# Attention's diagonal mask moved to TensorE, its shifts and biases to ScalarE, meta tokens in pieces, output weights split ahead, early Newton steps on GpSimd

## The chip, the cores and the metric

The kernel runs on one core of one Trainium2 chip. The metric is the device time of one execution in microseconds (us); three runs of the kernel before gave 3083.47, 3087.96 and 3088.3. The engines are PE (TensorE, with its weight loads), DVE (VectorE), ACT (ScalarE), POOL (GpSimd) and SP (SyncE, which issues nearly all DMAs here).

## The reference

One layer of a hybrid encoder over T = 2064 tokens (16 learned meta tokens and 2048 of input), width 1024, float32:

```python
p = rms_norm(h, g1) @ w_in                       # columns for three head groups
oa = rg_lru_group(...)                           # 256 wide, a linear recurrence
ob = forgetting_attention_group(q, k, v, f)      # 8 heads of 64
oc = rwkv7_group(...)                            # 256 wide, a matrix recurrence
h += rms_norm(concat(oa, ob, oc) @ w_out, g2)
f = causal_dwconv3(rms_norm(h, g3) @ ffn_up)     # 2 x 2816 columns
h += rms_norm((gelu(gate) * val) @ ffn_down, g4)

# attention of one head, c = cumsum(log_sigmoid(f + bias)):
s = q @ k.T + (c[:, None] - c[None, :])          # q scaled by 1/8
p = softmax(where(kpos <= qpos, s, -inf)); o = p @ v
```

The meta tokens are dropped at the end.

## The kernel before, in words

**Stages.** The projection runs in three parts of tokens, each over all 24 column groups ("units", 25 turns of a loop in a part); float32 operands are split into a high and a low float32r part and multiplied in three products (`mm3`, L166). Weights are split in the first part and kept in DRAM scratch for the other two. Beside it run the recurrences, sums for the up projection (`up_sums`, at every second unit of parts two and three, its DMAs queued behind the unit's weight load by `issue_after`), and, at the end, the recurrences' tail overlaps attention. Then come attention (`Attn`), the output projection by token tiles (`w_out_tile`: tile 0 has two meta tokens, sixteen more have 128 rows), the up projection and the down projection.

**What sets the order.** Each engine executes its own queue in order. The queues are filled by a planner that takes instructions by the program's order as priority and by a model of their times, so later work whose data is ready fills places that earlier work leaves: output tiles 0 to 6 stand among attention's second half. `issue_after` pins an instruction behind another in its queue. Tiles 7 and 8 are held until attention is nearly through.

**Attention.** Two halves: token blocks 0 and 1 for all eight heads, then blocks 2 and 3. One step is one head and one block of 512 queries, in two passes. `maxima` multiplies each of four query tiles with keys in pieces of at most 512 columns (L545, PSUM tile `mx`, two banks, three from head 5 of the first half on), and DVE reduces each piece to a column of `mc` (L548); the diagonal's last 128 columns go through a DVE operation that adds the mask `future` and takes the maximum, with a read of its accumulator (L551). Then DVE makes the shift column `sh` (L558, L559), PE transposes it (L563), DVE writes it into four rows of `q2` (L574), against four rows of ones in the keys, and DVE makes the bias of the exponentials (L566). `weights` makes scores (L673, L674), exponentials on ACT (L678, nine buffers `p`), values (L696) and denominators, added three times in four on POOL (L717). Maxima run two steps ahead of weights. `tick` counts clock steps, one per two key tiles, and at given delays runs the denominator's DMA round trip (`scr_den`, `dcol`, `rb`).

**Meta tokens.** `meta` computes attention of the first 16 tokens for all heads in one go between the two halves, in five of the nine `p` buffers.

**Output projection.** `w_out_load` loads eight slices of 512 KB, splits each by ACT (L162) and DVE (L163) and keeps them, once the recurrences' memory is free. A tile's two PSUM banks are squared and summed by ACT, `rstd_from` (L85 to L90) finds the reciprocal root by three Newton rounds of two DVE operations on one column, and DVE scales and adds; a second such norm follows for the next stage. From tile 8 on, `rstd_root` takes a square root on ACT instead.

## Time and profile before

| | |
|---|---|
| median of three runs | 3087.96 us (3083.47 to 3088.3) |
| profiled execution | 3087.03 us, span 3085.3 us |
| PE busy | 2905.6 us, 94% |
| DVE busy | 2127.9 us, 69% |
| ACT busy | 1447.5 us, 47% |
| POOL busy | 1317.4 us, 43% |
| mean granted PE clock | 0.964 |

The profile is one execution. A row of a grouped view reads: line, engine, operation, output<-inputs, shapes, count | busy us, mean ns of one | idle time of the engine just before, and who ended it. A row of waits reads: who waited <- for whom: us in total, times, longest. A busy PE may be waiting inside its pipeline, since the ends of its matmuls are modelled. The stages are about: projection to 885 us, attention to 1600, remaining output tiles to 1715, up projection to 2600, down projection to the end.

### The profile page before, as it was taken

How to read it: one execution, taken by the hardware profiler on the slowest of the kernel's cores; microseconds unless marked ns; L12 is line 12 of the kernel's file. 1: busy time of each engine (PE TensorE's matmuls, PEld its weight loads, DVE VectorE, ACT ScalarE, POOL GpSimd, SP SyncE). 2: the span in 40 equal slices, each digit the busy share in tenths (PEclk: the TensorE clock that was granted, in tenths of full speed). 3: DMA queues.
4: the chain of work that ended last, by engine and by line, in shares of the span. 5: the costliest groups of instructions: out<-in, count | busy, mean ns of one | idle time of the engine just before them, and what ended most of it. 6: DMA issues, size and time to landing. Idle time of an engine off the chain costs nothing.

```text
span 3085.3 us, 52708 instructions
## 1 busy us (share of the span) xinstructions
PE 2905.6 (94%) x18470; PEld 2485.8 (81%) x18470; DVE 2127.9 (69%) x4349; ACT 1447.5 (47%) x2783; POOL 1317.4 (43%) x1491
## 2 busy tenths in 40 slices
PE   7999999999989878898989899999999999999998
PEld 6998899888866544565458899999999998787876
DVE  5268544766677867777745788788778776547766
ACT  4245322444335534445534656666566665324333
POOL 1001121122134645546742457445645534556665
PEclk9999999999978979999999999999999999999999
DMA  6776457466653345445235555566777765435444
GB/s 216 244 229 215 148 176 221 153 219 219 192 134 78 91 112 126 109 112 119 61 112 185 166 175 176 178 196 213 216 211 212 217 193 164 167 103 174 145 163 143
DMA packets 463210, 515.78 MB, mean 167 GB/s; under 512 B 84977, under 2 KB 355003, under 8 KB 461393
## 3 DMA queue, kind: packets, MB, share of 16 engines
q1 hardware_dynamic: 462560, 512.03, 55.5%
q8 instruction: 145, 2.38, 0.3%
q14 instruction: 121, 0.98, 0.1%
q0 software_dynamic: 384, 0.39, 0.0%
HBM read 360.73 MB, written 151.56 MB: 166 GB/s over the span
## 4 chain that ended last, share of the span: by engine, by line
PE 39%; DMA 5%; DVE 5%; POOL 3%; issue 2%; ACT 1%; SPq 0%; POOLq 0%; DVEq 0%; ACTq 0%
PE psu L168 9%; PE psu L169 9%; PE psu L170 8%; PE psd L170 2%; PE psd L169 2%; PE psd L168 2%; DMA u<-scr_ff 1%; PE po L696 1%; DMA xt<-scr_h 1%; PE pswo L168 1%; PE pswo L169 1%; PE pswo L170 1%; DVE fo L1571 1%; PE sc L673 1%; DVE uw L1571 1%
## 5 line engine op out<-in xcount | busy, mean ns | idle before, releaser
L168 PE MATMUL psu<-xo,uw 128*128 128x344 f32 x1848 | 591.3, 324 | 16.2 <-ACT xo L1570 6.9
L169 PE MATMUL psu<-xo,uw 128*128 128x344 f32 x1848 | 594.1, 322 | 0.5 <-DVE xo L1571 0.5
L170 PE MATMUL psu<-xo,uw 128*128 128x344 f32 x1848 | 584.3, 320 | 0.0
L170 PE MATMUL psp<-xh,wl 128*128 128x384 f32 (+2 forms) x1152 | 379.1, 330 | 3.8 <-DMA wl<-scr_wk 3.8
L168 PE MATMUL psp<-xh,wh 128*128 128x384 f32 (+2 forms) x1152 | 380.2, 330 | 2.3 <-DMA wh<-scr_wk 2.3
L169 PE MATMUL psp<-xl,wh 128*128 128x384 f32 (+2 forms) x1152 | 377.6, 328 | 0.0
L168 PEld LDWEIGHTS psu<-xo,uw 128*128 128x128 f32 x1848 | 348.1, 189 | 19.5 <-ACT xo L1570 7.1
L1571 DVE TENSOR_TENSOR uw<-uq,uw 128x512 fp32r<-128x512 f32 x341 | 311.1, 918 | 65.3 <-ACT uw L1570 62.4
L169 PEld LDWEIGHTS psu<-xo,uw 128*128 128x128 f32 x1848 | 349.2, 189 | 1.1 <-DVE xo L1571 1.0
L170 PEld LDWEIGHTS psu<-xo,uw 128*128 128x128 f32 x1848 | 347.6, 189 | 0.0
L1570 ACT ACTIVATE uw<-uq 128x512 fp32r<-128x512 f32 x462 | 288.0, 627 | 113.0 <-PE psu L170 53.8
L678 ACT ACTIVATE p<-sc,bias 128x512 f32<-128x512 f32 (+4 forms) x352 | 197.8, 590 | 238.2 <-PE sc L674 181.7
L1701 DVE SCALAR_TENSOR_TENSOR uy<-psu,ffn_cols,uy 128x342 f32<-128x342 f32 (+1 forms) x396 | 223.8, 566 | 67.3 <-ACT uy L1699 65.9
L717 POOL TENSOR_TENSOR acc<-acc,p 128x512 f32<-128x512 f32 (+3 forms) x208 | 223.8, 1082 | 65.2 <-DVE acc L717 40.4
L1707 POOL TENSOR_TENSOR uy<-uy,uy 128x342 f32<-128x342 f32 (+1 forms) x132 | 138.5, 1049 | 256.3 <-DVE uy L1701 72.1
L170 PEld LDWEIGHTS psp<-xh,wl 128*128 128x128 f32 x1152 | 219.5, 191 | 13.3 <-issue 6.3
L1571 POOL TENSOR_TENSOR uw<-uq,uw 128x512 fp32r<-128x512 f32 x121 | 175.6, 1451 | 125.9 <-ACT uw L1570 102.8
L168 PEld LDWEIGHTS psp<-xh,wh 128*128 128x128 f32 x1152 | 219.6, 191 | 8.5 <-issue 3.5
L169 PEld LDWEIGHTS psp<-xl,wh 128*128 128x128 f32 x1152 | 219.3, 190 | 6.8 <-issue 4.8
L548 DVE TENSOR_REDUCE mc<-mx 128x1 f32<-128x400 f32 (+6 forms) x320 | 171.7, 553 | 67.3 <-PE mx L545 62.5
L1571 DVE TENSOR_TENSOR fo<-u,fo 128x896 fp32r<-128x896 f32 x88 | 109.7, 1247 | 122.4 <-ACT fo L1570 122.4
L1570 ACT ACTIVATE fo<-u 128x896 fp32r<-128x896 f32 x88 | 81.1, 922 | 206.2 <-POOL u L1817 111.7
(460 smaller groups left out, 6474.0 us busy)
## 6 DMA issues: line engine op xcount, KB each, us to landing
uq<-scr_us SPq DMA_DIRECT2D x220, 256.0 KB
uq<-in_ffn_up_dram SPq DMA_DIRECT2D x209, 256.0 KB
wl<-scr_wk SPq DMA_DIRECT2D x48, 512.0 KB
wh<-scr_wk SPq DMA_DIRECT2D x48, 512.0 KB
u<-scr_ff SPq DMA_DIRECT2D x88, 256.0 KB
scr_ff<-uy SPq DMA_DIRECT2D x110, 171.0 KB
raw<-in_w_in_dram SPq DMA_DIRECT2D x24, 512.0 KB
scr_wk<-wh SPq DMA_DIRECT2D x24, 512.0 KB
```

The costliest lines, as they stand in the source:

```text
L168: nc.tensor.matmul(out, ah, bh, start=first, stop=False, skip_group_check=more)
L169: nc.tensor.matmul(out, ah, bl, start=False, stop=False, skip_group_check=more)
L170: nc.tensor.matmul(out, al, bh, start=False, stop=last, skip_group_check=more)
L548: self.reduced = nc.vector.tensor_reduce(mc[:rows, i, ci : ci + 1], ps[:rows, :full], axis=AX.X, op=ALU.max)
L673: nc.tensor.matmul(ps[:rows, :w], k1[:, ks : ks + rows], q1[:, c0:n], start=True, stop=False)
L678: last = nc.scalar.activation(p[:rows, :w], ps[:rows, :w], AF.Exp, bias=bias[:rows, j : j + 1])
L696: mm = nc.tensor.matmul(po[at : at + 64, c0:n], v1[:rows, j], p[:rows, : n - c0], start=start and i < 2, stop=end and i + 2 >= len(group), ...
L717: eng.tensor_tensor(a, ps_[0][0][:rows, c0:n] if start and i == 1 else a, p[:rows, : n - c0], op=ALU.add)
L1570: core.nc.scalar.activation(hi, src, AF.Copy)
L1571: (eng or core.nc.vector).tensor_tensor(lo, src, hi, op=ALU.subtract)
L1701: stt(y[:, :n], src[:, i : n + i], cw[:, 44 * i + cc : 44 * i + cc + 1], y[:, :n], op0=ALU.mult, op1=ALU.add)
L1707: core.pooled = nc.gpsimd.tensor_tensor(v[:, :n], g[:, :n], v[:, :n], op=ALU.mult)
```

## The change

- **Mask.** The last piece of a query tile gets a second matmul, a bfloat16 identity times a bfloat16 mask, into its last 128 columns; DVE reduces the whole piece. The mask operation, its accumulator read and `junk` go. Where the diagonal is a piece of its own, a reduction takes the place of the mask operation alone.
- **Shift.** `sh` is the plain maximum; four transposes put its columns side by side into one row, and one ACT operation negates it, subtracts the reference (`ncref`) and writes one row of `q2`. One row of ones in the keys instead of four.
- **Bias.** The same expression on ACT.
- **Meta tokens.** `meta` is a generator of six pieces, advanced at every odd clock step, in tiles of its own, which lie below a `pad` of the size of the output stage's memory.
- **Output weights.** `w_out_split` loads and splits them in the projection's second part, at odd units, and stores both parts in scratch; `w_out_load` issues 16 loads.
- **Newton steps.** With `core.apart` (output tiles 0 to 7), the six steps of `rstd_from` run on GpSimd.

```diff
@@ rstd_from
+        if apart:
+            nc.gpsimd.tensor_scalar(t, y, hx, y, op0=ALU.mult, op1=ALU.mult)
+            nc.gpsimd.tensor_scalar(y, t, 1.5, y, op0=ALU.add, op1=ALU.mult)
+            continue
         stt(t, y, hx, y, op0=ALU.mult, op1=ALU.mult)
         stt(y, t, 1.5, y, op0=ALU.add, op1=ALU.mult)
@@ attn_consts, gate_block
+    core.futureb, core.identb = (c.tile([P, P], BF16, name=s) for s in ("futureb", "identb"))
...
+    nc.scalar.activation(core.ncref[:, js].rearrange("p j h -> p (j h)"), ps[0:1, :w], AF.Copy, scale=-1.0)
@@ Attn
-    ONES = 4
+    ONES = 1
@@ maxima
-                ps = self.mx()
-                nc.tensor.matmul(ps[:rows, : e - a], q3[:, qo : qo + rows], k2[:, a:e], start=True, stop=True)
-                full = min(e, prior) - a
-                if full > 0:
-                    self.reduced = nc.vector.tensor_reduce(mc[:rows, i, ci : ci + 1], ps[:rows, :full], axis=AX.X, op=ALU.max)
-                if e == prior + rows:
-                    junk = self.t([P, P], "mj")
-                    nc.vector.tensor_tensor_reduce(
-                        junk[:rows, :rows], ps[:rows, full : full + rows], core.future[:rows, :rows],
-                        1.0, NEG, ALU.add, ALU.max, mc[:rows, i, 5:6],
+                ps, last = self.mx(), e == prior + rows
+                nc.tensor.matmul(ps[:rows, : e - a], q3[:, qo : qo + rows], k2[:, a:e], start=True, stop=not last)
+                if last:
+                    nc.tensor.matmul(
+                        ps[:rows, prior - a : e - a], core.identb[:], core.futureb[:], start=False, stop=True
                     )
+                self.reduced = nc.vector.tensor_reduce(
+                    mc[:rows, i, ci : ci + 1], ps[:rows, : e - a], axis=AX.X, op=ALU.max
+                )
                 yield None
         sh = self.t([P, 4], "sh")
-        rows = qt[0][1]
-        nc.vector.tensor_reduce(sh[:rows, :nq], mc[:rows, :nq], axis=AX.X, op=ALU.max)
-        nc.vector.tensor_scalar(
-            sh[:rows, :nq], sh[:rows, :nq], -1.0, core.cref[:rows, ref, h : h + 1], op0=ALU.mult, op1=ALU.subtract
-        )
+        nc.vector.tensor_reduce(sh[:], mc[:], axis=AX.X, op=ALU.max)
         ps = self.mx()
-        nc.tensor.transpose(ps[:nq, :rows], sh[:rows, :nq], core.ident[:rows, :rows])
-        self.shift(q2.rearrange("p (i q) -> p i q", q=P), ps[:nq, :rows])
+        for i in range(nq):
+            nc.tensor.transpose(ps[0:1, P * i : P * i + P], sh[:, i : i + 1], core.ident[:])
+        nc.scalar.activation(q2[64:65], ps[0:1], AF.Identity, scale=-1.0, bias=core.ncref[:, ref, h : h + 1])
         bias = self.t([P, NKT], "bias", bufs=self.AHEAD + 1)
-        nc.vector.tensor_scalar(
-            bias[:], core.ccol[:, :, h], -1.0, core.cref[:, ref, h : h + 1], op0=ALU.mult, op1=ALU.add
+        nc.scalar.activation(
+            bias[:], core.ccol[:, :, h], AF.Identity, scale=-1.0, bias=core.cref[:, ref, h : h + 1]
         )
@@ meta
-        new = lambda shape, dt: self.t(shape, "p", dt, self.NP)
+        new = lambda shape, dt: pool.tile(shape, dt, name=core.n("mt"), tag=core.n("mt"))
...
+        yield
@@ tick
+        if self.clock % 2:
+            with self.core.tc.issue_after(self.reduced.ins):
+                next(self.beside, None)
@@ run
-                self.meta()
+                self.beside = self.meta(pool)
@@ w_out
+def w_out_split(core, pool, w_out, scr):
+
+    for k in range(KD):
+        hi, lo = (pool.tile([P, D], F32R, tag="nt_x", name=core.n("wo")) for _ in range(2))
+        load_parts(core, (pool, "nt_x", None), w_out[k * P : (k + 1) * P, :], hi[:], lo[:])
+        for i, t in enumerate((hi, lo)):
+            core.nc.sync.dma_start(scr["wo"][k, i], t[:].bitcast(F32))
+        yield
...
-        load_parts(core, (pool, "wx", None), w_out[k * P : (k + 1) * P, :], wh[:, k], wl[:, k])
+        for i, t in enumerate((wh, wl)):
+            nc.sync.dma_start(t[:, k].bitcast(F32), scr["wo"][k, i])
@@ hybrid_block_kernel
+            split_out = w_out_split(core, pools["nt"], a["w_out"], scr)
...
-                    if part and i % 2 == 0:
+                    if part and (i % 2 == 0 or part == 1 and i > 1):
                         with tc.issue_after(core.loaded.ins):
-                            next(sums, None)
+                            next(split_out if i % 2 else sums, None)
...
-            at.run()
+            pool(p1b, "pad", 1, **right).tile([P, 24832], F32, name="pad")
+            at.run(pool(p1b, "mt", 1, **right, **early))
...
+            core.apart = True
+            w = w_out_load(core, wp, scr)
...
                 banks.wide = core.root = i >= LATE - 1
+                core.apart = not core.root
```

More of the change, by code (lines that the diff above doesn't have):

```diff
@@ L333, in scratch @@
         "us": dr.tile([NFF, P, 4 * 512], F32, name="scr_us"),
+        "wo": dr.tile([KD, 2, P, D], F32, name="scr_wo"),
         "wk": dr.tile([3 * D // P + 1, 2, P, D], F32, name="scr_wk"),
@@ L354, in attn_consts @@
     c = core.const
-    core.future = c.tile([P, P], F32, name="future")
-    nc.gpsimd.memset(core.future[:], 0.0)
-    nc.gpsimd.affine_select(
-        out=core.future[:], in_=core.future[:], compare_op=ALU.is_ge, fill=NEG, base=0,
-        pattern=[[-1, P]], channel_multiplier=1,
-    )
+    core.future = c.tile([META, META], F32, name="future")
+    core.futureb, core.identb = (c.tile([P, P], BF16, name=s) for s in ("futureb", "identb"))
+    for t, n in ((core.future, META), (core.futureb, P)):
+        nc.gpsimd.memset(t[:], 0.0)
+        nc.gpsimd.affine_select(
+            out=t[:], in_=t[:], compare_op=ALU.is_ge, fill=NEG, base=0, pattern=[[-1, n]], channel_multiplier=1
+        )
+    nc.vector.tensor_copy(core.identb[:], core.ident[:])
     core.ones_row = c.tile([1, P], F32, name="ones_row")
@@ L366, in attn_consts @@
     core.cref = c.tile([P, NKT, NH], F32, name="cref")
+    core.ncref = c.tile([1, NKT, NH], F32, name="ncref")
     core.ctail = c.tile([NH, META], F32, name="ctail")
@@ L442, in __init__ @@
         self.clock, self.later, self.serial, self.added = 0, [], 0, 0
-        self.pending, self.loads, self.steps = None, [], []
+        self.pending, self.loads, self.steps, self.beside = None, [], [], iter(())
         self.turn = {"k": 1, "q2": 0, "q3": 0}
@@ L613, in meta @@
         self.shift(q2, ps[:NH, :META])
+        yield
         ps = eight(self.mx(), META)
@@ L622, in meta @@
         )
+        yield
         po, den = eight(self.mx(), 64), eight(self.mx(), 64)
@@ L787, in tick, with run @@
                 self.later.pop(0)[2]()
+        if self.clock % 2:
+            with self.core.tc.issue_after(self.reduced.ins):
+                next(self.beside, None)
     AHEAD = 2
-    def run(self):
+    def run(self, pool):
         ready = []
@@ L814, in run @@
         self.flush()
+        for _ in self.beside:
+            pass
         for _, _, f in self.later:
```

19 lines of the change are left out of this document (10 added, 9 removed).

## The prediction

> **What bounds the kernel now.** I read the page's slices first, then the busy time by stage, then the waits. The slices are forty equal parts of the span, in tenths:
>
> ```profile
> span 3085.3 us, 52708 instructions
> ...
> DVE  5268544766677867777745788788778776547766
> ...
> PEclk9999999999978979999999999999999999999999
> ```
>
> All of the change's work but one edit lies in slices 11 to 20, the attention; outside it PE is at 9 nearly everywhere and its clock is full. The clock sinks in slices 11 to 14, where DVE stands at 7 to 8. By stage (busy time of PE, weight loads, DVE, ACT and POOL in order, each with its count, then the clock, the DMA share and GB/s): attention's first half beside the recurrences, its second half beside the first output-projection tiles, the remaining tiles.
>
> ```profile
> 885.00:1145.00 260.00, 216.71 (x1839) 146.48 (x1835) 208.85 (x682) 116.84 (x254) 123.89 (x199) 0.82 0.43 100
> 1145.00:1600.00 455.00, 413.74 (x1744) 243.09 (x1743) 320.68 (x753) 212.33 (x376) 257.38 (x284) 0.95 0.41 101
> 1600.00:1715.00 115.00, 103.22 (x484) 86.09 (x483) 68.45 (x110) 56.11 (x127) 27.19 (x23) 0.96 0.61 196
> ```
>
> First half: DVE 209 of 260 us (80%), PE at clock 0.82, so PE is not full and DVE is the nearest thing to a bound. Second half: PE 91% with its waits counted in, DVE 70%, POOL 57%, ACT 47%: no engine is full; an in-order PE waits for others in turn. What it waits for (the first row is of the first half, the others of the second):
>
> ```profile
> PEld mx L545 <- DVE q L574: 10.1, 6, 5.0
> ...
> ACT p L678 <- PE sc L674: 129.7, 87, 6.6
> PEld sc L673 <- ACT p L678: 29.6, 55, 5.2
> PEld mx L545 <- DVE mc L548: 12.7, 21, 1.8
> ...
> PEld mx L545 <- DVE mc L551: 8.1, 3, 4.7
> ```
>
> So DVE stops the maxima through their PSUM banks (12.7 + 8.1), and the exponentials stop the scores (29.6): 50.4 us in the second half.
>
> **The change part by part.** One (head, block) step is four query tiles; each half has 16 steps. What DVE sheds, first half:
>
> ```profile
> L551 DVE CUSTOM_DVE_ANT_0 mj<-mx,future 128x128 f32<-128x128 f32 x64 | 17.5, 277 | 7.1 <-PE mx L545 7.1
> L574 DVE TENSOR_TENSOR q<-mx,ident 4x512 fp32r<-4x512 f32 x16 | 10.9, 682 | 6.2 <-PE mx L563 5.8
> L566 DVE TENSOR_SCALAR bias<-ccol,cref 128x17 f32<-128x17 f32 x17 | 9.5, 567 | 0.1
> L559 DVE TENSOR_SCALAR sh<-sh,cref 128x4 f32<-128x4 f32 x16 | 7.8, 487 | 0.1
> L551 DVE DVE_READ_ACCUMULATOR2_ANT mc<- 128x1 f32 x64 | 5.1, 79 | 0.0
> ```
>
> and second half, with the reductions that stay:
>
> ```profile
> L548 DVE TENSOR_REDUCE mc<-mx 128x1 f32<-128x512 f32 x112 | 75.0, 679 | 38.0 <-PE mx L545 37.7
> L548 DVE TENSOR_REDUCE mc<-mx 128x1 f32<-128x400 f32 x64 | 35.4, 561 | 10.1 <-PE mx L545 9.9
> L551 DVE CUSTOM_DVE_ANT_0 mj<-mx,future 128x128 f32<-128x128 f32 x64 | 17.1, 272 | 0.3 <-PE mx L545 0.3
> L559 DVE TENSOR_SCALAR sh<-sh,cref 128x4 f32<-128x4 f32 x16 | 13.1, 819 | 0.2
> L90 DVE SCALAR_TENSOR_TENSOR rsv<-rsv 128x1 f32<-128x1 f32 x21 | 12.2, 581 | 0.3
> L89 DVE SCALAR_TENSOR_TENSOR rs<-rs 128x1 f32<-128x1 f32 x21 | 11.8, 560 | 0.7
> L574 DVE TENSOR_TENSOR q<-mx,ident 4x512 fp32r<-4x512 f32 x16 | 10.9, 682 | 2.1 <-PE mx L563 1.6
> L163 DVE TENSOR_TENSOR wol<-raw,woh 128x1024 fp32r<-128x1024 f32 x8 | 9.9, 1243 | 5.9 <-ACT woh L162 5.8
> L89 DVE SCALAR_TENSOR_TENSOR rsv<-rsv 128x1 f32<-128x1 f32 x21 | 9.7, 463 | 0.6
> L566 DVE TENSOR_SCALAR bias<-ccol,cref 128x17 f32<-128x17 f32 x15 | 6.8, 454 | 1.1 <-ACT p L678 1.1
> L90 DVE SCALAR_TENSOR_TENSOR rs<-rs 128x1 f32<-128x1 f32 x21 | 5.0, 237 | 0.3
> L551 DVE DVE_READ_ACCUMULATOR2_ANT mc<- 128x1 f32 x64 | 5.0, 78 | 0.0
> L548 DVE TENSOR_REDUCE mc<-mx 128x1 f32<-128x128 f32 x16 | 4.5, 281 | 4.3 <-PE mx L545 4.2
> ```
>
> *Mask, shift, bias.* Removed from DVE: 17.5 + 5.1 + 10.9 + 9.5 + 7.8 = 50.8 us in the first half, 17.1 + 5.0 + 10.9 + 6.8 + 13.1 = 52.9 in the second. Added: the diagonal's 128 columns go into the reduction. A column costs (679 - 561)/112 = 1.05 ns, so three tiles of a step grow by 0.135 us, and the fourth, whose diagonal is a piece of its own, gets a reduction of 0.281: 0.69 a step, 11.0 a half. Net 39.8 and 41.9 us.
>
> *Output weights and Newton steps*, second half only: 9.9 for the split and 12.2 + 11.8 + 9.7 + 5.0 = 38.7 for the steps of seven full tiles. DVE's second half falls by 90.5, from 320.7 to 230; its first from 208.9 to 169.
>
> What comes on other engines:
>
> ```profile
> L745 ACT ACTIVATE acc<-mx 1x512 f32<-1x512 f32 x32 | 18.5, 577 | 5.9 <-PE mx L744 4.8 <-PE sc L674 0.8
> L678 ACT ACTIVATE p<-sc,bias 16x16 f32<-16x16 f32 x32 | 8.3, 259 | 13.3 <-PE sc L674 5.2 <-DVE acc L717 3.6 <-PE po L696 2.1
> ...
> L563 PE MATMUL mx<-ident,sh 128*4 128x128 f32 x32 | 9.2, 289 | 13.1 <-DVE mc L538 7.1 <-DVE rwgsm L76 4.9 <-DVE sh L559 1.2
> L1537 PE MATMUL pst<-ident,xt 128*128 128x128 f32 x56 | 7.2, 272 | 0.0
> ...
> L717 POOL TENSOR_TENSOR acc<-acc,p 128x512 f32<-128x512 f32 x120 | 157.2, 1310 | 41.4 <-DVE acc L717 24.4 <-ACT p L678 8.6 <-DVE rsv L85 2.4
> L1010 POOL TENSOR_SCALAR rwsg<-rwsg 128x256 f32<-128x256 f32 (+1 forms) x9 | 3.5, 385 | 208.1 <-ACT rwsg L1009 208.1
> ```
>
> ACT: a shift is one row of 512, 0.577; a bias of 17 columns is nearest to the 16-column row, 0.26 (bounds 0.2 and 0.577): 0.84 a step, 13.4 a half, on an engine below 50%. It stands in ACT's queue behind exponentials, and the next maxima bank waits for it (a rival below). The Trainium skill, "ScalarE: Activation LUTs", section "Rules for kernel authors", would keep additions and multiplications on VectorE. The trace differs for the shift, 577 ns against 682 on DVE; by the rule the shift would cost ACT more than DVE saves, by the row less.
>
> PE: four mask matmuls and three more transposes a step, seven of 128 columns. In a dense run 56 such took 7.2 us, 0.129 each; alone one shows 0.289. Seven are 0.9 to 2.0 us a step, 14.5 to 32 a half. I take 14.5, for they stand among other matmuls; in the first half PE's slack hides them, in the second I pay them. If that slack is gone, the first half's 14.5 is paid too.
>
> POOL: 96 steps (eight tiles, two norms, six). Its nearest operation, 256 columns, takes 0.385; a column alone takes no more, and I say 0.25 (bounds 0.1, a quarter of that row, and 0.385): 24 us on 257 of 455, hidden by POOL's idle 43%; without that cover 24. Each waits behind additions of 1.31 us, and for the pair of output banks the first norm waits with it.
>
> *From DVE's time to the end's.* First half: at the same 80% DVE's 169 us would need 211, 49.5 less; if the recurrences' serial chain sets the pace, nothing. I take the middle, -25. Second half: at the same 70% it would be -128, which PE's 414 busy of 455 rules out; the least is +14.5 (PE's addition, no relief). I take the row of the waits: the 50.4 us go, the 14.5 come, -36.
>
> *Meta tokens.* Their chain ran in one piece between the halves and held DVE behind PE (first row below; the other two are the output weights', next part):
>
> ```profile
> DVE p L631 <- PE mx L626: 3.3, 1, 3.3
> ...
> L162 ACT ACTIVATE woh<-raw 128x1024 fp32r<-128x1024 f32 x8 | 8.5, 1057 | 9.7 <-DMA raw<-in_w_out_dram 9.7
> ...
> raw<-in_w_out_dram SPq DMA_DIRECT2D x8, 512.0 KB
> ```
>
> Cut in pieces, with tiles of their own instead of five of the nine exponential buffers, I count -3 (0 to -8). The first output tile reads them and comes some twelve clock steps later; late with it are the filler matmuls, which the stretch without output tiles can take: 0.
>
> *Output weights ahead.* In the second third of the projection 8 x 1.5 MB of DMA and 8 x (1.06 + 1.24) us of ACT and DVE come in. That stage, and the heaviest one:
>
> ```profile
> 300.00:600.00 300.00, 295.49 (x2533) 268.19 (x2532) 157.65 (x410) 103.45 (x202) 55.75 (x93) 0.98 0.56 175
> ...
> 100.00:200.00 100.00, 100.00 (x550) 95.88 (x549) 40.54 (x73) 33.87 (x59) 1.43 (x3) 1.00 0.77 254
> ```
>
> The eight loads stand at every other of 16 units out of 25, some 190 of 300 us: 12.6 MB are 66 GB/s more, 241 in all, under the 254 at which PE was 100% busy. ACT 34% and DVE 53% hide the rest: +3 (0 to +13, if PE waits 1.6 us for each of eight loads). Later 16 loads of 512 KB replace eight, 8.4 MB, at 254 GB/s 33 us instead of 16.5, in one burst in the queue of the heads' loads and denominators: +4 (0 to +16.5).
>
> The sum, against the profiled execution's 3087.0 us (span 3085.3; 0.9 below the median of the three runs): 3087.0 - 25 - 36 - 3 + 3 + 4 = **3030**.
>
> **The rivals.**
> *DVE sets both halves.* The 80% of the first half speaks for it, POOL and PE in the second against: -49.5 there and -70 (all 50.4 us and about half of PE's 41 idle ones, PE's addition hidden), so 3087 - 49.5 - 70 - 3 + 7 = 2971.
>
> *Relief that nobody waits for.* The waits change hands; only those for removed instructions go: 10.1 + 8.1 = 18.2, against 14.5 for PE: 3087 - 18.2 + 14.5 - 3 + 7 = 3087. For it: ACT's 129.7 us of waiting for scores, which DVE does not cause.
>
> *The shift in ACT's queue, the slower side.* ACT waits 129.7/87 = 1.5 us for scores, then takes 0.68; a shift behind one such exponential holds its bank 2.2 us and PE with it: 32 x 2.2 = 70, 3030 + 70 = 3100. It decides from 57/32 = 1.8 us a shift upwards. Against it: three banks after the first five heads, and two steps of lead.
>
> *Newton steps late on POOL.* Six steps, each behind an addition, are 6 x 1.56 = 9.4 us, against 6 x 0.40 on DVE; eight tiles whose banks wait that long: 56, so 3030 + 56 = 3086. Against it: output tiles are filler that may slip. The Trainium skill, "GPSIMD Engine Reference", section "Engine selection", gives elementwise work to VectorE as about twice as fast. The steps' means of 237 to 581 ns on DVE, beside POOL at work, make the trace doubtful of that here.
>
> **How the numbers follow.** Forecast 0.55 (own range 3000 to 3065, the halves' -25 and -36 moved by half of either), DVE bound 0.10, relief unused 0.14, shift in ACT's queue 0.13, late Newton steps 0.08. About 0.2% is what a measurement of this kernel tells from no change: 3082 and 3094. Faster: 0.54 + 0.10, and 0.10 from the others' lower sides, 0.74. Same 0.14, mostly the third and fifth. Slower 0.12, nearly all the ACT rival. The range 2975 to 3096 leaves out half of the first rival and most of the slower one.
>
> **What would show it.** Right: DVE busy near 169 and 230 us in the two halves, no wait of maxima for a shift above 1 us in the mean, clock above 0.82 in the first half, projection and FFN stages as long as before. The mask's matmuls should show about 0.13 us of spacing, the moved steps 0.25 us. Wrong: attention as long as before with DVE emptier (third case); maxima waiting for ACT (fourth); output tiles waiting for reciprocal roots (fifth); PE waiting for projection weights, or denominators waiting for DMA around the output weights' burst, by more than 20 us.

## The result and the profile after

The changed kernel takes 3068.11 us (median of five runs, 3064.79 to 3073.51) beside 3083.47 (median of five) for the kernel before on the same chip: a ratio of 0.995, 95% interval 0.9934 to 0.9966. It is faster by some 15 us; 57 were forecast. The profiled execution took 3073.51 us, 13.5 us less in span than the one before.

The page of the changed kernel, its span and two rows of slices:

```profile
span 3071.8 us, 52793 instructions
...
DVE  5268645656667785556635788888778786547766
...
PEclk9998999999988898999999999999999999999999
```

DVE sank by one to two tenths in slices 15 to 20 (counted from 0, as in the prediction), and the lowest digit of PE's clock is 8 instead of 7, but the span moved by less than a fifth of a slice (77 us). To find where the time is, I cut attention at three events that both traces have: the last matmul of the projection (880.4 us before, 896.3 after), the start of the 112th of 352 exponentials (1170.6 and 1147.6; the first half has 112), and the last exponential (1576.8 and 1565.0). "First half" and "second half" mean these stretches from here on. The stage view of the kernel before (columns as in the prediction: PE, weight loads, DVE, ACT, POOL busy, clock, DMA share, GB/s):

```profile
880.40:1170.60 290.20, 245.17 (x1987) 162.90 (x1987) 231.73 (x732) 131.91 (x278) 135.51 (x211) 0.82 0.45 108
1170.60:1576.80 406.20, 372.63 (x1578) 218.58 (x1580) 292.53 (x691) 193.50 (x349) 245.97 (x268) 0.97 0.40 96
```

and of the changed kernel, the second half whole and then in three pieces (until the first output matmul, until output tile 6 is through, and the rest):

```profile
896.30:1147.60 251.30, 225.57 (x1995) 151.47 (x1995) 201.71 (x536) 139.43 (x302) 130.76 (x208) 0.90 0.44 103
1147.60:1565.00 417.40, 399.15 (x1778) 233.25 (x1779) 234.62 (x475) 209.01 (x381) 282.33 (x354) 0.96 0.46 117
1147.60:1202.70 55.10, 47.53 (x194) 23.45 (x194) 32.39 (x75) 17.39 (x35) 20.86 (x26) 0.75 0.85 251
1202.70:1403.60 200.90, 198.84 (x895) 125.10 (x894) 111.20 (x231) 99.37 (x180) 136.69 (x190) 1.00 0.43 109
1403.60:1565.00 161.40, 152.78 (x692) 84.69 (x692) 91.03 (x172) 92.25 (x167) 124.78 (x139) 0.99 0.36 82
```

The account: projection +15.9, first half -38.9, second half +11.2, output tiles that remain +1.1, the rest of the kernel -2.9; together the 13.5. The first half fell in step with DVE: it is 80% busy in both (231.73 of 290.2, 201.71 of 251.3). The second half grew although DVE lost 58 us there. PE's idle time in it was 406.2 - 372.6 = 33.6 us before and is 18.3 now, while PE's busy time rose by 26.5. Between 1203 and 1404 us PE stands at 99% and DVE at 55%: PE has only 2 us of idle time left there that a further relief of DVE could give back.

Part of the 26.5 has only moved. The first output tile (the one that reads meta tokens) started at 1153 us, 18 us ahead of the first half's last exponential, and 43 of its 48 matmuls lay in the first half; now it starts at 1202.7, 55 us behind. The output tiles' matmuls in one and the same 200 us, before and after:

```profile
1200.00:1400.00 200.00, 71.54 (x280) 52.42 (x281) 13.35 (x20) 7.55 (x22) 0.98 0.44 111
```

```profile
1200.00:1400.00 200.00, 80.69 (x321) 54.54 (x322) 15.97 (x24) 8.24 (x24) 1.00 0.44 109
```

At 0.25 us each, 43 matmuls are 10.8 us (an estimate from the two rows). If they cost as much in either half, then on equal work the first half is 28 us shorter and the second neither shorter nor longer; if they cost nothing in the first half, where PE has idle time, it is the full 38.9. What holds the first output tile shows in SP's queue: it must load the mixed rows behind the store of the meta tokens' output. Before:

```profile
1145.80 0.63 SPq L633 DMA_DIRECT2D scr_mix<-p  x1
1148.63 0.38 SPq L161 DMA_DIRECT2D raw<-scr_mix  x1
```

After:

```profile
1190.49 0.62 SPq L640 DMA_DIRECT2D scr_mix<-mt  x1
1198.51 0.58 SPq L165 DMA_DIRECT2D raw<-scr_mix  x1
```

The operations that were added, by their form, from 1145 to 1600 us:

```profile
L556 PE MATMUL mx<-futureb,identb 128*128 128x128 bf16 x61 | 14.4, 237 | 0.0
...
L90 POOL TENSOR_SCALAR rsv<-rsv 128x1 f32<-128x1 f32 x21 | 12.9, 613 | 3.0 <-DVE rsv L87 2.0
...
L568 ACT ACTIVATE q<-mx,ncref 1x512 fp32r<-1x512 f32 x16 | 10.8, 678 | 13.7 <-PE mx L567 13.3
...
L90 POOL TENSOR_SCALAR rs<-rs 128x1 f32<-128x1 f32 x21 | 7.2, 344 | 5.0 <-DVE rs L87 4.2 <-DVE acc L725 0.3
...
L570 ACT ACTIVATE bias<-ccol,cref 128x17 f32<-128x17 f32 x14 | 4.6, 326 | 0.5
```

And two waits of the same stretch (who <- for whom: us in total, times, longest):

```profile
DVE mc L559 <- PE mx L554: 70.0, 54, 5.2
...
DVE pswo L1522 <- POOL rs L91: 10.2, 6, 2.4
```

DVE now waits 70 us for the maxima's matmuls, 55.7 before: more of the waiting is DVE's for PE.

### The profile page after: what moved, and what is told of

Its sections match the earlier page's. It is cut to its first block, busy times and chain, and to the rows that moved or that the text cites. A ratio compares the mean times of both kernels' runs of the same rounds, so it can differ in the third digit from the quotient of the medians.

```text
span 3071.8 us, 52793 instructions
## 1 busy us (share of the span) xinstructions
PE 2921.6 (95%) x18694; PEld 2495.2 (81%) x18694; DVE 2054.8 (67%) x3934; ACT 1482.3 (48%) x2853; POOL 1358.8 (44%) x1589
## 5 line engine op out<-in xcount | busy, mean ns | idle before, releaser
L559 DVE TENSOR_REDUCE mc<-mx 128x1 f32<-128x512 f32 (+6 forms) x352 | 190.3, 565 | 100.9 <-PE mx L554 75.8
```

The lines of the kernel that those rows point to most:

```text
L559: self.reduced = nc.vector.tensor_reduce(mc[:rows, i, ci : ci + 1], ps[:rows, : e - a], axis=AX.X, op=ALU.max)
```

## The experiments

All are edits of the changed kernel, timed on several chips, each beside the kernel before on its own chip. The table gives the first and second half as cut above and PE's busy and idle time in the second (one profiled execution each), and the ratio of the times to the kernel before with its 95% interval. Eight runs whose first half has the same work on every engine show it at 250.9 to 253.8 us, so 3 us there are no difference. The projection scatters more: 885.0 to 903.9 us in the twelve runs that have the split ahead in it (a_mask, below, is the twelfth).

| run | first half | second half | PE busy | PE idle | ratio |
|---|---|---|---|---|---|
| before | 290.2 | 406.2 | 372.6 | 33.6 | 1 |
| changed kernel | 251.3 | 417.4 | 399.2 | 18.3 | 0.995 (0.9934 to 0.9966) |
| a_nosplit | 250.9 | 420.8 | 397.2 | 23.6 | 0.9933 (0.9909 to 0.9957) |
| a_newton | 253.1 | 424.0 | 398.9 | 25.1 | 0.9968 (0.9952 to 0.9985) |
| a_meta | 260.1 | 417.4 | 389.4 | 28.0 | 0.997 (0.9954 to 0.9986) |
| a_mask2 | 265.4 | 411.3 | 387.6 | 23.7 | 0.9992 (0.9975 to 1.001) |
| a_pe4 | 274.9 | 406.6 | 392.6 | 14.0 | 1.0028 (1.0007 to 1.0049) |
| a_dve2 | 272.7 | 417.8 | 395.0 | 22.8 | 1.0018 (1.0001 to 1.0036) |
| a_nomask | 251.8 | 409.0 | 386.7 | 22.3 | 0.992 (0.99 to 0.994) |
| a_metafast | 253.8 | 434.2 | 397.3 | 36.9 | 1.0002 (0.998 to 1.0024) |
| a_two | 251.5 | 392.4 | 371.7 | 20.7 | 0.9879 (0.9841 to 0.9916) |
| a_attn | 272.3 | 400.0 | 376.9 | 23.1 | 0.9952 (0.9932 to 0.9973) |
| a_best | 252.7 | 405.3 | 387.0 | 18.3 | 0.9952 (0.9929 to 0.9975) |
| a_order | 253.8 | 430.4 | 404.9 | 25.6 | 1.0005 (0.999 to 1.002) |
| a_ordn | 251.0 | 423.9 | 398.5 | 25.4 | 0.9981 (0.9964 to 0.9997) |
| a_best2 | 261.3 | 409.0 | 387.3 | 21.7 | 0.9948 (0.9929 to 0.9967) |
| a_best3 | 283.8 | 396.3 | 373.1 | 23.2 | 0.9995 (0.9978 to 1.0011) |
| a_pe4h2 | 251.8 | 424.5 | 403.9 | 20.6 | 0.9949 (0.993 to 0.9969) |
| a_bn | 258.8 | 405.9 | 384.0 | 22.0 | 0.9934 (0.9913 to 0.9956) |

One thing in the second half is not the same in all of these runs: PE's granted clock until the first output matmul. It is 0.75 in the changed kernel and in a_two, 0.72 in a_nosplit, 0.78 in a_newton and a_metafast, 0.81 in a_dve2 and a_meta, and 0.91 to 0.93 in a_pe4, a_mask2 and a_nomask, whose second halves are 6 to 11 us shorter than the changed kernel's. If PE's 47.5 busy us there went by the clock alone, 0.93 instead of 0.75 would take 9 us off (an estimate). So up to some 9 us between two second halves need not be the price of the edit.

### Single parts undone

**Output weights.**

```diff
-        for i, t in enumerate((wh, wl)):
-            nc.sync.dma_start(t[:, k].bitcast(F32), scr["wo"][k, i])
+        load_parts(core, (pool, "wx", None), w_out[k * P : (k + 1) * P, :], wh[:, k], wl[:, k])
...
-            split_out = w_out_split(core, pools["nt"], a["w_out"], scr)
...
```

> The changed kernel with one part undone: the output weights are split into their two parts at the start of attention's second half again (eight loads of 512 KB, ScalarE and VectorE there), not ahead in the projection. BURST theory: the 16 loads of 512 KB (issued from 1164 to 1189 us, 366 GB/s) and the queue behind them cost the second half's start 15 to 25 us, so this run is 3043 to 3055 us, and the stretch from the 113th to the last exponential falls from 402 to 380-390 us. FULL PE theory: PE is full from 1200 to 1400 us whatever DMA does, so only the projection's stay of about 5 us comes back: 3060 to 3068, stretch 398 to 406 us. The forecast's own prices: minus 3 and minus 4, plus up to 9.9 for VectorE: 3061 to 3071.

Without the burst the second half is 420.8 us, no shorter: the burst theory falls. The projection ends at 887.0 us instead of 896.3, a difference inside its scatter, and the two ratios' intervals overlap.

**Newton steps.**

```diff
-            core.apart = True
+            core.apart = False
...
-                core.apart = not core.root
+                core.apart = False
```

> The changed kernel with one part undone: the Newton steps of the first seven tiles' norms on VectorE again. FULL PE theory: VectorE stands at 55% there and nobody waits for it: 3068 within 5 us, stretch from the 113th to the last exponential 402 within 5. The forecast: the steps are 38.7 of 90.5 us of VectorE's relief, so 43% of its 36 us, 15 us, are lost: 3083. LATE STEPS theory (GpSimd's steps of 0.34 to 0.61 us hold the output banks): faster, 3050 to 3060, and the output tiles' wait for the roots (10.2 us now) gone.

40 us more of DVE's busy time in the second half (274.2 beside 234.6) are worth 0.0018 of the time, 6 us, at intervals that overlap; the forecast's share for them was 15. That GpSimd's steps hold the banks is refuted too: their return to DVE gains nothing.

**Meta tokens.**

```diff
-                self.beside = self.meta(pool)
+                for _ in self.meta(pool):
+                    pass
...
```

> The changed kernel with one part undone: the meta tokens run in one piece between the halves, in the exponentials' buffers, so that their ten loads needn't wait for the recurrences' memory. BURST theory: these loads, which now start at 1150 us only, hold the queue of keys, queries and denominators at the start of the second half; without that 5 to 10 us less: 3058 to 3063, and the 3rd block's first exponentials come without the stop at 1150 to 1165. The forecast: 3 us more, 3071. FULL PE theory: nothing, 3065 to 3071.

The first half gets 9 us longer, the second stays at 417.4, although its first output matmul now comes 21 instead of 55 us behind the 112th exponential. By the ratios it is 6 us, at intervals that overlap.

**Mask.** In the first of these two runs attention itself began late, for a reason of memory that the second's expectation tells (ratio 1.0275, 1.0247 to 1.0303); the second has the mask alone.

```diff
...
-                    nc.tensor.matmul(
-                        ps[:rows, prior - a : e - a], core.identb[:], core.futureb[:], start=False, stop=True
-                    )
...
+                if full > 0:
+                    self.reduced = nc.vector.tensor_reduce(mc[:rows, i, ci : ci + 1], ps[:rows, :full], axis=AX.X, op=ALU.max)
                 if last:
...
+                    nc.vector.tensor_tensor_reduce(
+                        ps[:rows, full : full + rows], ps[:rows, full : full + rows], core.futuref[:rows, :rows],
+                        1.0, NEG, ALU.add, ALU.max, mc[:rows, i, 5:6],
                     )
...
```

> The changed kernel with one part undone: the diagonal's mask on VectorE again (its fused add-and-max and the read of the accumulator), so four of the seven added TensorE matmuls of a step are gone (8.3 us a half at 0.129 each). FULL PE theory: the second half pays PE, so it is 8 us shorter (stretch from the 113th to the last exponential 394), the first half, which VectorE sets, 5 to 7 us longer: together 3064 to 3068. The forecast: first half 7 us longer (11.6 of 39.8 us of VectorE's relief), second 2 us longer: 3077. BURST theory: says nothing of this part beyond the 7 us: 3070 to 3075.

> The run a_mask once more, with the fused add-and-max writing back into the scores' own bank and no tile of its own: in a_mask the first key tile of attention waited for the recurrences' memory (the wait of GpSimd's memset for the recurrences' TensorE work, 34.6 us at the last, and the first exponential at 1083 instead of 924 us), so its time says nothing of the mask. FULL PE theory: PE loses 8.3 us a half, VectorE gets 11 us a half: 3 to 12 us less than the changed kernel. The forecast: 9 us more. VECTORE theory: 15 to 22 us more.

```profile
903.90:1169.30 265.40, 229.35 (x1936) 154.22 (x1936) 207.08 (x663) 140.29 (x302) 132.81 (x210) 0.86 0.43 100
1169.30:1580.60 411.30, 387.59 (x1708) 229.40 (x1710) 238.75 (x570) 209.87 (x379) 279.57 (x354) 0.98 0.46 118
```

The two halves disagree in sign: with the mask on DVE the first is 14 us longer, the second 6 us shorter, and by the ratios the whole is 13 us slower. That is a first hint that the halves have different bounds, though the second's 6 us are no more than the clock (0.93 here) can give.

### Work for one engine added or taken away

DVE alone, then PE alone, then PE in the second half alone, then the mask on neither engine:

```diff
-                self.reduced = nc.vector.tensor_reduce(...)
+                for _ in range(2 if last else 1):
+                    self.reduced = nc.vector.tensor_reduce(...)
```

> The changed kernel with work for VectorE alone added: the reduction of each query tile's last piece of scores is made twice (same result). 64 more reductions a half of 0.28 to 0.68 us, some 32 us a half, about what the change took from VectorE there by the forecast (39.8 and 41.9 us). FULL PE theory: VectorE has the room (209 of 266 us, 227 of 402): at most 10 us more in all. The forecast's own prices (25 us for 39.8 in the first half, 36 us for 90.5 in the second): 20 + 13 = 33 us more. VECTORE theory: 50 us more, most of both additions.

```profile
887.30:1160.00 272.70, 235.50 (x2002) 153.06 (x2001) 218.70 (x607) 140.63 (x302) 130.55 (x210) 0.88 0.43 101
1160.00:1577.80 417.80, 395.00 (x1771) 231.00 (x1772) 264.91 (x532) 209.46 (x381) 281.31 (x355) 0.98 0.45 114
```

Added to DVE: 17 us of busy time in the first half, 30 in the second. Paid: 21.4 us in the first half (again 80%: 218.70 of 272.7), 0.4 in the second; by the ratios 21 us in all. The clock until the first output matmul is a little higher here, 0.81, which may hide some 3 us (an estimate as above). So DVE's added work is paid in full in the one half and hardly at all in the other. A second reduction also holds its PSUM bank longer, so this run alone doesn't part DVE's load from the time that a bank is held.

```diff
-                if last:
+                for again in range(4 if last else 0):
                     nc.tensor.matmul(..., core.identb[:], core.futureb[:], start=False, stop=again == 3)
```

> The changed kernel with work for TensorE alone added: the mask's matmul on the diagonal is issued four times instead of once (the mask is added four times; the result is the same). 64 x 3 = 192 more matmuls of 128 columns in each half, 24.8 us a half at 0.129 each, and no other engine has more to do. FULL PE theory (attention is bound by PE: 739 us busy of 793): the whole addition is paid in the second half and most of it in the first, where PE was 89% busy: 40 to 50 us more than the changed kernel, about 3110. VECTORE theory (the relief is not paid because VectorE's maxima are still last): PE's idle time (54 us in attention) takes most of it: up to 15 us more.

```profile
890.00:1600.00 710.00, 53.52 (x512) 29.98 (x512) 0.95 0.44 109
```

This row is the mask's line alone. The changed kernel's:

```profile
890.00:1600.00 710.00, 30.46 (x128) 12.86 (x128) 0.94 0.45 114
```

384 more, each behind another of its kind, cost 23.1 us of PE, 0.060 each and not the 0.129 of the forecast. The ratio is 0.0078 above the changed kernel's, 24 us, between the two expectations. The first half grew by 23.6 us, twice the 11.5 added there, and the second shrank by 10.8, which neither theory had. The run's own rows, the first half and the stretch until the first output matmul:

```profile
901.30:1176.20 274.90, 238.50 (x2216) 162.51 (x2215) 200.23 (x553) 141.20 (x302) 133.32 (x211) 0.90 0.44 106
1176.20:1214.90 38.70, 33.35 (x183) 18.47 (x183) 25.08 (x51) 14.19 (x29) 15.86 (x20) 0.91 0.96 269
```

DVE is busy for 73% of this first half, not 80: DVE's busy time does not set that half by itself. The three extra matmuls stand between a bank's filling and its reduction, so DVE gets each bank later (its waits for the maxima's matmuls are 23.1 us there, 12.8 in the changed kernel); that this is what lengthens the half is argued, not shown. Part of the second half's 10.8 us is a moved border: the first output matmul comes 39 us behind the 112th exponential instead of 55. Both halves together are 12.8 us longer. The next run leaves the first half as it is:

```diff
+                times = 0 if not last else 4 if b > 1 else 1
```

> The mask's matmul four times instead of once in the steps of attention's second half alone (192 more matmuls of 128 columns, 11.5 us by the 60 ns that one more took of PE's busy time in the run with both halves). FULL PE theory: first half as in the changed kernel (251 us from the last projection matmul to the 112th exponential), second half 8 to 12 us longer, total 3076 to 3082. Rival (PE's price is nothing there, and what counts is when the first half ends against the recurrences): total within 4 us of the changed kernel.

```profile
891.00:1142.80 251.80, 225.43 (x2007) 151.73 (x2007) 199.95 (x536) 139.55 (x302) 131.01 (x208) 0.90 0.44 103
1142.80:1567.30 424.50, 403.93 (x1959) 243.02 (x1960) 235.64 (x475) 210.03 (x381) 283.70 (x354) 0.98 0.46 116
```

The second half is 7.1 us longer with 4.8 us more of PE busy, yet the timed ratio is that of the changed kernel: a price between 0 and 1 that this run doesn't settle.

```diff
...
-                if last:
-                    nc.tensor.matmul(
-                        ps[:rows, prior - a : e - a], core.identb[:], core.futureb[:], start=False, stop=True
-                    )
...
```

> The changed kernel without the mask on the scores of which the maxima are taken (neither engine does it): the 128 matmuls of the mask are left out, so a shift is the largest score over some later keys too, and the exponentials' own mask is left as it is. Nothing else changes. FULL PE theory: 16.5 us of PE's work (0.129 each) goes, all of it paid: 12 to 17 us less than the changed kernel. VECTORE theory: 0 to 5 us less. The forecast: 8.3 us less in the second half, nothing in the first.

```profile
885.00:1136.80 251.80, 220.16 (x1928) 149.90 (x1927) 199.28 (x543) 140.07 (x302) 132.99 (x210) 0.88 0.45 104
1136.80:1545.80 409.00, 386.68 (x1716) 231.79 (x1718) 237.53 (x469) 209.26 (x379) 279.97 (x355) 0.97 0.46 120
1136.80:1188.50 51.70, 45.65 (x209) 23.99 (x210) 32.72 (x73) 23.64 (x43) 25.80 (x30) 0.93 0.86 262
```

PE's 5 us less in the first half give nothing, 12.5 us less in the second give 8.4, just as the forecast had it (8.3 and nothing), and by the ratios it is 9 us, at intervals that overlap. It looks like the mirror image of DVE's, but the last row's clock, 0.93 instead of 0.75, could give the second half's 8.4 us as well. Then the output tiles' own work:

```diff
+            if s < META + 6 * P:
+                nc.tensor.matmul(ps[:rows], mh[:, k, :rows], wh[:, k, cs], start=k == 0, stop=False)
+                nc.tensor.matmul(ps[:rows], ml[:, k, :rows], wh[:, k, cs], start=False, stop=k == KD - 1)
+                continue
```

> The changed kernel with one of the three products of the output projection (high part by the weights' low part) left out in its first seven tiles, those that run beside attention's second half: 112 matmuls of 512 columns, some 25 us of PE's work, less; the output is that much less exact. FULL PE theory for the stretch of the output tiles (1203 to 1404 us, PE 99% busy): this stretch is shorter by most of it and the total falls by 18 to 25 us. Rival (the exponentials' or the maxima's chain sets the second half and the output tiles only fill its gaps): the stretch is shorter, but what follows it is longer, and the total falls by less than 8 us.

```profile
894.30:1145.80 251.50, 223.30 (x1996) 150.81 (x1995) 202.52 (x537) 139.27 (x302) 131.59 (x208) 0.90 0.44 103
1145.80:1538.20 392.40, 371.74 (x1666) 211.75 (x1667) 242.19 (x475) 209.15 (x380) 285.98 (x354) 0.97 0.49 125
```

27.4 us of PE's busy time less, 25.0 us of the second half less, at the changed kernel's clock of 0.75 until the first output matmul, and the timed kernel shows it (0.9879). This is the cleanest price of PE's work in the second half. So the output tiles don't fill gaps for nothing; they are part of what the second half is made of.

### When the first output tile comes

After the burst theory fell, a second one blamed its lateness. Every clock step instead of every second for the meta tokens' pieces:

```diff
-        if self.clock % 2:
-            with self.core.tc.issue_after(self.reduced.ins):
-                next(self.beside, None)
+        with self.core.tc.issue_after(self.reduced.ins):
+            next(self.beside, None)
```

> The changed kernel with the meta tokens' pieces issued at every clock step of the planner instead of every second one. LATE FILLER theory (what the second half lost): the store of the meta tokens' output comes at 1190 us and the first output tile's load and first matmul only behind it (1198, 1203 us), 55 us after the first half's last exponential; until then PE stands at 86% busy and clock 0.75, and afterwards it is 99% full for 200 us. So with the pieces twice as fast the first output matmul comes 10 to 20 us earlier behind the 112th exponential (35 to 45 us), and the time falls by 5 to 12 us. Rival (the lateness is covered, as the run with meta in one piece suggests, whose first output matmul came after 21 us and whose time was no better): no change beyond 3 us.

The first output matmul came 46.8 us behind the 112th exponential, 8 earlier, and the second half got 17 us longer, all of it PE's idle time (36.9). The tile that reads meta tokens after the others:

```diff
-            for i, (f, rows) in enumerate(FFN_TILES):
+            tiled = list(enumerate(FFN_TILES))
+            for i, (f, rows) in tiled[1:7] + tiled[:1] + tiled[7:]:
```

> The changed kernel with the first output tile (two rows, the only tile that reads meta tokens) taken after the sixth of the others, so that the tile that comes first needs nothing of the meta tokens. No work is added or removed. LATE FILLER theory: the first output matmul comes with the output weights' first loads (1165 to 1180 us instead of 1203, that is 15 to 30 us behind the 112th exponential instead of 55), PE's stop at 86% and clock 0.75 is shorter, and the total falls by 8 to 15 us. FULL PE theory (the work alone counts): the output tiles begin and end earlier, the exponentials behind them take as much longer, and the total moves by less than 4 us.

> The last edit, and the output weights split in attention again. LATE FILLER theory: both add up, minus 8 to 15 and minus 5: 3048 to 3055 on the changed kernel's 3068. FULL PE theory: only the 5 us of the projection: 3060 to 3066. If the burst of 8.4 MB were what holds the tiles, this run would gain 10 us more than the one with the burst.

Both expectations were wrong in their premise. The first output matmul came later still, 66 and 85 us behind, since the other tiles need the first half's last heads (in a_order their loads are issued at 1212.5 us, behind the last store of those heads at 1210.2), and the second half took 430.4 and 423.9 us. The lateness theory isn't borne out by any run: earlier in a_meta (21 us) brought nothing, earlier in a_metafast a loss, later here a loss of 13, and of 3 beside a_nosplit's 420.8.

### The attention part alone, and combinations

Mask, shifts and bias alone (the edits of a_nosplit, a_newton and a_meta together):

> The mask, the shifts and the bias alone as in the changed kernel: output weights split in attention, Newton steps on VectorE and meta tokens in one piece as in the kernel before. The forecast: its two halves without Newton steps and split, 3087 minus 25 minus some 17 (the 50.4 us by 41.9 of 90.5, and PE's 14.5 added: 23 - 14.5 = 9 at the least), so 3045 to 3053. LATE FILLER theory: the first output matmul is back within 10 us of the first half's last exponential; the first half keeps 30 to 39 us of its gain, the second half pays PE's addition (10 to 15 us): 3058 to 3070. By the three single undoings (plus 5, plus 6, minus 5 us against the changed kernel): 3075 to 3080.

```profile
888.50:1160.80 272.30, 239.86 (x2082) 159.33 (x2082) 210.06 (x563) 146.96 (x311) 133.83 (x211) 0.87 0.47 113
1160.80:1560.80 400.00, 376.88 (x1692) 225.07 (x1692) 274.67 (x547) 209.30 (x380) 251.38 (x268) 0.98 0.41 101
```

The whole gain of the change is there, 0.9952 beside 0.995. It comes as 17.9 us in the first half (the meta tokens' piece and 36 matmuls of the first output tile are in it) and 6.2 in the second. By this comparison the other three parts together gain nothing: they take 21 us more out of the first half and put 17 into the second, and add some 5 us to the projection (its end is at 894 us in the mean of twelve runs with the split ahead, at 888 in the eight without, and either group spreads over 15 us or more).

The combinations, in the order a_best, a_best2, a_best3, a_bn, each with the edits that its expectation names; "the last edit" of a_best2 is the whole of a_ordn:

> Three single edits together on the changed kernel: output weights split in attention again, meta tokens' pieces at every clock step, and no mask on the scores of which the maxima are taken (the shift is then the largest score over some later keys too). If they add up: minus 5, minus 5 to 12, minus 9 against the changed kernel: 3042 to 3052. If the second half is full either way, the first two are worth nothing here: 3058 to 3064.

> The last edit, and no mask on the scores of which the maxima are taken (the shift is then the largest score over some later keys too). FULL PE theory: PE's work is what the second half is made of, so the mask's 18 us of PE's busy time give 8 to 9 us as in the run without the mask alone, whatever the tiles' order: 3050 to 3058. LATE FILLER theory: 3038 to 3048.

> Output weights split in attention and meta tokens in one piece as in the kernel before, no mask on the scores of which the maxima are taken, Newton steps on GpSimd: 3055 to 3062 by either theory (against the run with mask, shifts and bias alone, 0.9952 of the kernel before: minus 9 for the mask, minus 3 to 5 for the Newton steps).

> Output weights split in attention again and no mask on the scores of which the maxima are taken (the shift is then the largest score over some later keys too); meta tokens' pieces at every second step and the tiles in order, as in the changed kernel. If the single gains add up: 0.9933 and 0.992 against the changed kernel's 0.995 make 0.9903 of the kernel before, some 3054. If only one counts: 0.992 to 0.9935, 3060 to 3064.

None adds up; a_bn came out as if only one of its gains counted. Their medians lie at 3064 to 3082 us beside 3083 to 3087; the best, 0.9934, can't be told from the changed kernel. In two of them leaving out the mask made the first half longer, though PE has less to do there: 261.3 us in a_best2 beside 251.0 in a_ordn, 258.8 in a_bn beside 250.9 in a_nosplit. The runs don't show why, so that PE's work costs nothing in the first half is not the whole story. In a_best the two halves of attention are 658.0 us beside the changed kernel's 668.7, and the timed median doesn't show it. No version was shown to beat the changed kernel but a_two, which leaves a product out.

## Why the prediction was wrong

**First half, -25: right in direction, short in size.** It is 38.9 us shorter, 28 if the moved matmuls cost as much here as in the second half. DVE's share stayed at 80%, which is what the first rival said of this half, and a_dve2 gave time back at the same 80%. But a_pe4 made the half as long as a_dve2 did, with DVE at 73%. Whether DVE's load sets this half, or the time that a bank is held from its first matmul to its reduction, no run settles. The bounds held. DVE's busy time fell by 30 us and not by 39.8, to 201.7 and not to 169. The records of single operations did add up to 42 us less: the durations of DVE's small operations overlap in the records. In the kernel before, DVE's records add up to 2356 us and cover 2127.9. Over both halves its busy time fell from 231.7 + 292.5 to 201.7 + 234.6, by 88 us, where the forecast's sum of records had 130 and the trace's has 115. The Trainium skill ("Perfetto Trace Analysis", section "Optimizing Scalar/DVE Operations") says that such an operation's fixed data-access time shows in the profile at about twice what the engine is busy with it, as the acknowledgement of the write overlaps the next instruction; the two sums agree with it in direction.

**Second half, -36: the step that failed is "the 50.4 us go".** They were waits of the weight loads' queue for banks and exponentials, and they were taken as gain in full. Such a wait lies partly under the matmul that is still running: in the prediction's own stage row PE was idle for only 41.3 us (455.00 less 413.74), and in the second half as cut here for 33.6, so 50.4 couldn't go. PE's own waits for the same three causes, from 1145 to 1600 us before, were 26.8 us:

```profile
PE sc L673 <- ACT p L678: 11.6, 15, 4.7
...
PE mx L545 <- DVE mc L551: 9.4, 4, 4.3
...
PE mx L545 <- DVE mc L548: 5.8, 8, 1.6
```

Both queues' rows in the same stretch of the changed kernel:

```profile
PEld mx L554 <- DVE mc L559: 16.3, 32, 0.9
PEld sc L681 <- ACT p L686: 14.8, 43, 0.9
...
PE sc L681 <- ACT p L686: 3.4, 12, 0.5
...
PE mx L554 <- DVE mc L559: 2.4, 7, 0.7
```

So of the 50.4 us of the weight loads' waits 31.1 stayed; PE's own fell from 26.8 to 5.8, and with other waits that came in their place PE's idle time fell by 15.3. The term for PE's added work, 14.5, came out as a sum: PE's busy time rose by 26.5, which is 15.7 without the 10.8 that moved. Its parts are not settled, and that they meet the sum is partly luck. A mask matmul behind another costs 0.060 us and not 0.129, but that is not the price of the first one in a bank. The transposes have 0.153 each and not 0.129 (the row below, the changed kernel's transposes alone: 19.62 us for 128); the 32 of the kernel before took 9.2, so they added 5.2 a half and not 6.2. And PE's clock was 0.75 for the first 55 us.

```profile
885.00:1600.00 715.00, 19.62 (x128) 9.84 (x128) 0.94 0.45 113
```

-15.3 + 15.7 is nothing, and nothing is what the second half gave on equal work. The third case, "relief that nobody waits for", describes this half, as a_dve2 shows; its sum of 3087 missed because it gave the first half only 10.1 us of relief. In the table PE's busy time and the second half go together: the idle rest is 14 to 28 us in every edit but a_metafast.

**Meta tokens, -3; the first tile's lateness, 0.** In pieces they save 9 us of the first half (a_meta, one execution) and 6 by the ratios, at intervals that overlap. That the tile's lateness would cost nothing is neither refuted nor shown; with it 10.8 us of work went from one half into the other.

**Output weights, +3 and +4.** The projection's price is about 5 us by the two means, inside the bounds; the 15.9 of the one profiled execution are mostly scatter by that. The burst's +4 isn't seen: 417.4 with it, 420.8 without.

**Newton steps.** 0.34 to 0.61 us on GpSimd, 0.43 in the mean, and not 0.25; the mean is above the bound of 0.385. DVE's wait for them is 10.2 us. For operations with two inputs the Trainium skill ("GPSIMD Engine Reference", section "Engine selection") calls GPSIMD about twice as slow as VectorE, for one input roughly as fast as data can stream. The prediction left that condition out. The steps have two tensor inputs on VectorE and one on GpSimd. VectorE took 237 to 581 ns for the same steps, so a factor of two isn't what separates the two engines here. Since the fifth case priced the delay at 56 us, it is out: a_newton gained nothing.

**The shift in ACT's queue (the slower side).** 678 ns instead of 577, on a par with DVE's 682, and the bias 326 instead of 260. The changed kernel's waits of the maxima for it, from 885 to 1600 us:

```profile
PEld mx L554 <- ACT q L568: 3.8, 5, 1.9
...
PE mx L554 <- ACT q L568: 2.5, 3, 1.7
```

At 0.2 us a shift the case, which needed 1.8, is out.

**The rest.** In slices 11 to 14 DVE's digits are 7, 7, 8 and 6, not 7 to 8. FFN stages as long as before: right (-2.9). Clock above 0.82 in the first half: right, 0.90. "DVE near 230 us" in the second half: nearly met, 234.6, and yet without the gain. The range held the time; the likeliest case's own range ended 3 us short of it. Most of what gain there is comes from the first half's surplus over -25 and -3, 11 us of the 15.

## What to carry to other kernels

Before waits are counted as gain, read the engine's idle time in that stage from the stage view: no sum of waits of a queue that runs ahead of its engine can give more than that. Price each engine by stage with one run that adds or takes away some of its work there; here VectorE's added work was paid in the first half and hardly in the second, and TensorE's, taken out of the second half's output tiles, came back at 25.0 of 27.4 us. Read the granted clock of the stage in each run before its time is put down to the edit. When an edit moves a block of work across a stage's border, compare the stages on equal work.

## What the runs showed of the hardware that was not expected

- One more 128x128 bfloat16 matmul behind another of its kind costs 0.060 us of PE (a_pe4) though its record has 0.226 to 0.238. The Trainium skill, "TensorE: Matmul & The Clock Gate", section "Wait — 56ns, not 53.3ns?", gives 55.6 ns from start to start; the runs agree.
- The projection, with the split ahead in it, took 885.0 to 903.9 us, and the granted clock from the 112th exponential to the first output matmul was 0.75 in the changed kernel and 0.72 to 0.93 in the single edits. What sets either is open.
- Why PE idles 19 us more in a_metafast, why the first half of a_pe4 grows by twice what was added, and why a_best2 and a_bn have a longer first half with less work for PE, is open as well.
